# Five pairs of the gated MLP's first product computed by seven quarter products, and five row-pair sums of its last weights moved into the mixer

## The chip, the cores and the metric

The program runs on one core of a Trainium2 chip. The core has five engines that run side by side, each through its own queue of instructions: TensorE (PE in the profile; PEld is its weight load), VectorE (DVE), ScalarE (ACT), GpSimd (POOL) and SyncE (SP, which only issues transfers here). They wait for each other by semaphores. Data lies in SBUF, in 128 partitions; products arrive in PSUM, in banks of 512 columns of float32. The time is that of one execution on the device in microseconds, and the time before is the median of the runs shown.

## The reference

One layer of a streaming encoder on 512 tokens of 1024 channels, in float32: a mixer of four branches (differential attention, forgetting attention, a convolution module, a short gated convolution), a cross-attention, and a gated MLP. The change lies in the MLP, whose lines in the reference are these:

```python
hf = _rms_norm(x, norm_ffn_pre[l])
u = _dwconv_causal(hf @ w_up[l], ffn_dw[l]) + ffn_dw_b[l]
u_g, u_v = jnp.split(u, 2, axis=-1)
yff = (jax.nn.silu(u_g) * u_v) @ w_down[l]
x = x + _rms_norm(yff, norm_ffn_post[l])
```

`w_up` is 1024 x 5632, its first half for the gate, the second for the value; `w_down` is 2816 x 1024; the convolution along the tokens has three taps for each channel.

## The kernel before, in words

Each float32 product is made of three matmuls: every operand is split into a high part (a cast by ScalarE, the tiles `wh`, `hth`) and a low part (the rest, a subtraction by VectorE, the tiles `wl`, `htl`), and high x high, low x high and high x low are summed in PSUM (`mm3`). `split_weights` (L179 to L192) makes the parts of a weight tile of 128 x 1024; in the profile the cast is L190 and the subtraction L191.

The kernel is written as generators of jobs. `run_blocks` takes them in order, loads and splits the weights of the jobs ahead (three of them), and then runs the body of a job. A background list (`bg`) weaves smaller tasks in by an estimated clock. The order of the program's instructions on each engine is then that of the build; each engine works through its own queue strictly in order.

The up-projection is `up_jobs`. There are 22 pairs j of 128 gate and 128 value channels, so 44 jobs, one weight tile of 512 KB each (`wr`, loaded by SP). A job of the plain kind is `channel_major`: 8 blocks of 128 input channels, three matmuls each, 24 matmuls with 512 token columns. Then `done` makes the convolution: the first tap as a ScalarE activation with bias from PSUM into the tile `c`, the other two taps by VectorE from PSUM (`taps`, L594). After the value half of a pair, the gate is made by a Tanh on ScalarE (L1561) and two VectorE instructions (L1562 and L1564), which write a tile `qa` or `qb`. The first two pairs come while the normalised tokens `hth`, `htl` are still being transposed: their first halves of the tokens are computed ahead, and their second halves when `open_ffn` has opened the stage. A bank that holds a product is free for the next product but one only after its last tap.

The second product, `down_jobs`, already works with seven products for each 2 x 2 block of quarters. It needs sums and differences of the quarters of the weights and of the activations. Those of the weights are made by the class `Sums`: `load` fetches two rows of 128 x 1024 of `w_down`, `add` makes four VectorE additions of 128 x 512 (L542 to L545), `store` writes them to DRAM, from where the second product reads them. `up_jobs` does one step of these in each job from the seventh on, on ScalarE's DMA queue, for 11 pairs. Those of the activations are four GpSimd additions of 128 x 256 for each two pairs (`activation_sums`, L566 to L569), issued as soon as the second pair of the two is done.

The mixer is `mixer_jobs`: among others `vf_jobs`, `kv_blocks` and `gate_blocks`, jobs of the same kind with the attention tasks in the background. The residual of the tokens lies in four tiles `res` from the end of the mixer to the end of the kernel.

## Time and profile before

| | us |
|---|---|
| runs shown | 1057.01, 1057.06, 1056.11 (median 1057.01) |
| the profiled execution | 1055.79 |
| its span, first to last instruction | 1054.0 |
| TensorE busy | 1041.7 (99%) |
| VectorE busy | 807.1 (77%) |
| ScalarE busy | 501.9 (48%) |
| GpSimd busy | 184.3 (17%) |

In the profile a line of the timeline gives start, length, engine, line, operation, output and inputs, shape and count, and in brackets the idle time before it with what ended it. A matmul's length in the timeline overlaps the next one's, so what matmuls cost is read from start to start, as in the chain that ended last. Rows with `x11` and two numbers after the bar are groups: busy us and mean ns. The up-projection runs from about 696 us, where the first halves of the first two pairs stand, to about 938 us; the second product follows up to 1044 us.

### The profile page before, as it was taken

The page shows a single profiled execution, that of the slowest core. Times are in us where ns is not written, and L with a number is a line of the kernel's source. Part 1 is how long each engine was busy: PE and PEld are TensorE (multiplying, and loading weights), DVE is VectorE, ACT ScalarE, POOL GpSimd, SP SyncE. Part 2 cuts the span into 40 slices and gives each one's busy share as a digit, 9 for nine tenths or more (in the row PEclk, how much of TensorE's full clock was granted, in tenths as well). Part 3 has the DMA queues.
Part 4 walks back from the last instruction along what each step waited for, and adds up shares of the span by engine and source line. Part 5 has one row for each costly group of instructions (what it writes and reads, how often), then busy time and mean ns, then how long its engine had stood idle before and what let it go on. Part 6 is the DMA issues. An engine that isn't in the chain of part 4 may idle for free.

```text
span 1054.0 us, 14559 instructions
## 1 busy us (share of the span) xinstructions
PE 1041.7 (99%) x5295; PEld 886.8 (84%) x5295; DVE 807.1 (77%) x1280; ACT 501.9 (48%) x823; POOL 184.3 (17%) x309
## 2 busy tenths in 40 slices
PE   9999999999999999999999999999999999999996
PEld 8888888888888988888888899998888888888885
DVE  6899997668667467867487798777878777777795
ACT  5322222277465365655444566554333333355661
POOL 4000000300231233433011031121112111111001
PEclk9999999999999999999999999999999999999998
DMA  8854434742342353232359644135576676626662
GB/s 276 282 168 102 103 100 142 193 109 81 116 140 82 100 161 101 80 100 85 96 172 284 207 132 126 60 111 190 186 243 229 214 233 215 196 81 211 210 188 80
DMA packets 165373, 163.08 MB, mean 155 GB/s; under 512 B 6527, under 2 KB 136172, under 8 KB 165045
## 3 DMA queue, kind: packets, MB, share of 16 engines
q1 hardware_dynamic: 152995, 119.91, 38.0%
q0 software_dynamic: 5824, 19.03, 6.2%
q10 hardware_dynamic: 6482, 23.21, 5.7%
q8 instruction: 42, 0.69, 0.3%
q14 instruction: 30, 0.25, 0.1%
HBM read 139.03 MB, written 23.09 MB: 154 GB/s over the span
## 4 chain that ended last, share of the span: by engine, by line
PE 99%; DVE 0%; ACT 0%; issue 0%; POOL 0%; POOLq 0%; DVEq 0%; ACTq 0%
PE ps_mm L232 51%; PE ps_av L232 31%; PE ps_sc L232 8%; PE ps_tr L232 4%; PE ps_tr L236 2%; PE ps_mm L442 1%; PE ps_av L442 1%; PE ps_mm L384 0%; PE ps_sc L389 0%; DVE o L1710 0%; PE ps_tr L426 0%; POOL st_m L270 0%; POOLq L1816 0%; ACT hth L155 0%; ACT hth L432 0%
## 5 line engine op out<-in xcount | busy, mean ns | idle before, releaser
L190 ACT CAST wh<-wr 128x1024 fp32r<-128x1024 f32 (+1 forms) x142 | 148.8, 1049 | 273.3 <-PE ps_mm L232 175.0
L191 DVE TENSOR_TENSOR wl<-wr,wh 128x1024 fp32r<-128x1024 f32 (+1 forms) x142 | 178.5, 1258 | 79.0 <-ACT wh L190 78.8
L232 PE MATMUL ps_mm<-hth,wh 128*128 128x512 f32 (+1 forms) x592 | 221.1, 380 | 0.2 <-ACT hth L155 0.2
L232 PE MATMUL ps_mm<-htl,wh 128*128 128x512 f32 (+1 forms) x592 | 220.7, 379 | 0.0
L232 PE MATMUL ps_mm<-hth,wl 128*128 128x512 f32 (+1 forms) x592 | 220.6, 379 | 0.0
L232 PE MATMUL ps_av<-htl,wh 128*128 128x512 f32 (+1 forms) x352 | 131.8, 374 | 0.0
L232 PE MATMUL ps_av<-hth,wh 128*128 128x512 f32 (+1 forms) x352 | 131.8, 374 | 0.0
L232 PE MATMUL ps_av<-hth,wl 128*128 128x512 f32 (+1 forms) x352 | 131.6, 374 | 0.0
L232 PEld LDWEIGHTS ps_mm<-hth,wh 128*128 128x128 f32 x592 | 109.6, 188 | 20.4 <-ACT hth L155 0.8
L232 PEld LDWEIGHTS ps_mm<-hth,wl 128*128 128x128 f32 x592 | 109.5, 188 | 20.1
L232 PEld LDWEIGHTS ps_mm<-htl,wh 128*128 128x128 f32 x592 | 109.6, 188 | 19.7
L665 DVE SCALAR_TENSOR_TENSOR y<-y,par,y 128x482 f32<-128x482 f32 (+29 forms) x120 | 83.3, 735 | 0.1
L232 PEld LDWEIGHTS ps_av<-hth,wl 128*128 128x128 f32 x352 | 66.1, 188 | 11.9
L232 PEld LDWEIGHTS ps_av<-hth,wh 128*128 128x128 f32 x352 | 66.2, 188 | 11.8
L232 PEld LDWEIGHTS ps_av<-htl,wh 128*128 128x128 f32 x352 | 66.0, 188 | 11.7
L1613 DVE TENSOR_TENSOR wl<-dw,wh 128x1024 fp32r<-128x1024 f32 x32 | 40.2, 1262 | 13.3 <-ACT wh L1612 13.1
L1612 ACT CAST wh<-dw 128x1024 fp32r<-128x1024 f32 x32 | 33.4, 1051 | 23.4 <-PE ps_tr L232 7.9
L1058 POOL TENSOR_SCALAR fbias<-ck,cq 128x128 f32<-128x128 f32 (+3 forms) x32 | 28.2, 888 | 63.0 <-DVE st L1065 59.7
L1561 ACT ACTIVATE th<-c 128x512 f32<-128x512 f32 x22 | 13.9, 632 | 48.0 <-DVE c L594 48.0
L155 ACT CAST pth<-ps_tr 128x512 fp32r<-128x512 f32 (+3 forms) x56 | 23.5, 448 | 24.7 <-PE ps_tr L236 24.6
L594 DVE SCALAR_TENSOR_TENSOR c<-ps_mm,par,c 128x510 f32<-128x510 f32 (+1 forms) x44 | 32.8, 744 | 0.7
L156 DVE TENSOR_TENSOR ptl<-ps_tr,pth 128x512 fp32r<-128x512 f32 (+3 forms) x56 | 27.5, 512 | 5.9 <-ACT pth L155 5.4
(493 smaller groups left out, 2132.5 us busy)
## 6 DMA issues: line engine op xcount, KB each, us to landing
wr<-in_w_up SPq DMA_DIRECT2D x44, 512.0 KB
wr<-in_w_in SPq DMA_DIRECT2D x38, 512.0 KB
wr<-in_w_gate SPq DMA_DIRECT2D x32, 512.0 KB
wp<-in_w_down ACTq DMA_DIRECT2D x22, 512.0 KB
sums<-wp ACTq DMA_DIRECT2D x22, 512.0 KB
dw<-sums SPq DMA_DIRECT2D x44, 256.0 KB
wr<-in_w_branch SPq DMA_DIRECT2D x16, 512.0 KB
wide<-in_w_out SPq DMA_DIRECT2D x12, 512.0 KB
```

The lines of the kernel that those rows point to most:

```text
L155: A.copy(hi, ps)
L156: V.tensor_tensor(lo, ps, hi.bitcast(F32), ALU.subtract)
L190: order(A.copy(hi, raw[:, :n]))
L191: low.tensor_tensor(lo, raw[:, :n], hi.bitcast(F32), ALU.subtract)
L232: PE.matmul(ps, lhs, rhs, start=start, stop=stop)
L236: PE.transpose(ps, x, ident[:n, :n])
L442: keep(PE.matmul(banks[c][:, :S // 2], w[p == 1][:, k, c * P:(c + 1) * P], ht[p == 2][:, i * 4 + k, :S // 2], start=(i, p, k) == (0, 0, 0) ...
L594: ins = V.scalar_tensor_tensor(dst[:, s:], src[:, :S - s], w(k), dst[:, s:], ALU.mult, ALU.add)
L665: ins = V.scalar_tensor_tensor(dst[:, s:], src[:, :S - s], pc("conv_dw", k * 4 + j), dst[:, s:], ALU.mult, ALU.add)
L1058: G.tensor_scalar(bias[:, :w], ck[j][:, :w], -1.0, cq[:, qt, head:head + 1], ALU.mult, ALU.add)
L1612: A.copy(hi, x)
L1613: V.tensor_tensor(lo, x, hi.bitcast(F32), ALU.subtract)
```

## The change

It has four parts.

First, the pairs 4, 7, 10, 13 and 16 (`SEVEN_AT`) are computed by seven products instead of plain ones. The 128 gate and 128 value columns are the two columns of a 2 x 2 block, the two halves of the input channels its rows, and the two halves of the tokens the other side. Each product is 12 matmuls with 256 token columns. The weights' sums and differences are four VectorE additions of 128 x 512 (L1706 to L1709) on the raw tiles `wg` and `wv`, which come by the same two loads of 512 KB; there are four splits (three of 128 x 1024, one of 128 x 512). The tokens' sums and differences are the same for all five blocks and are made once by `token_terms`: eight GpSimd additions of 128 x 1024, with four splits by ScalarE and VectorE, when the first two pairs are done. A seven-product pair is woven with the plain pair after it (`seven_jobs`). Its results are put together in a tile `u` by four ScalarE copies and three VectorE additions from PSUM; the convolution then reads `u`.

Second, five of the eleven row pairs of `w_down` get their sums in the mixer (`down_early`, `EARLY`), in tiles `y8` and on SP's queue; the other six stay in the up-projection, from pair 5 on.

Third, the sums of the activations are issued from pair 18 on (`quart_sums`), for one or two pairs of quarters at a time, and GpSimd is used as before. The tiles of the terms take the place of the residual, which is written to DRAM (`kept`) and read back in the second product.

Fourth, the gate is a Silu on ScalarE and one VectorE multiplication.

The core of the diff:

```diff
+SEVEN_AT = (4, 7, 10, 13, 16)
+EARLY = 5
...
+        early = down_early()
+        for job in vf_jobs(vf):
+            yield job
+            yield next(early)
...
+        else:
+            SP.dma_start(ns.kept[t * P:(t + 1) * P, :], ns.out[t])
...
+    def token_terms():
+
+        tok = [slice(i * S // 2, (i + 1) * S // 2) for i in range(2)]
+        b = {}
+        for k, t in ((0, 0), (0, 1), (1, 1), (1, 0)):
+            ks = slice(4 * k, 4 * k + 4)
+            x = b[k, t] = ring(name="b").rearrange("p (k c) -> p k c", k=4)
+            G.tensor_tensor(x, ns.hf[0][:, ks, tok[t]].bitcast(F32), ns.hf[1][:, ks, tok[t]].bitcast(F32), ALU.add)
+            if (k, t) == (0, 1):
+                G.tensor_tensor(b[0, 0], x, b[0, 0], ALU.subtract)
+            elif (k, t) == (1, 1):
+                G.tensor_tensor(b[0, 1], x, b[0, 1], ALU.subtract)
+                G.tensor_tensor(x, x, b[0, 0], ALU.subtract)
+            elif (k, t) == (1, 0):
+                G.tensor_tensor(x, x, b[1, 1], ALU.subtract)
+        for i, n in ((0, (0, 0)), (1, (1, 1)), (2, (0, 1)), (3, (1, 0))):
+            split(b[n], *ns.terms[i])
...
+        def gated(c, j):
+            A.activation(c[:, 0], c[:, 0], AF.Silu)
+            V.tensor_tensor(ns.quart[j // 2][:, j % 2 * 2:j % 2 * 2 + 2].rearrange("p a b -> p (a b)"), c[:, 0],
+                            c[:, 1], ALU.mult)
...
-                th = ns.fp.tile([P, S], F32, tag="th", name="th")
-                A.activation(th, c[:, 0], AF.Tanh, scale=0.5)
-                V.scalar_tensor_tensor(th, th, 1.0, c[:, 0], ALU.add, ALU.mult)
...
-                if j % 2:
-                    activation_sums(*x, G)
...
+            def product(ps, name, b, first=True):
+                hi, lo = w[name]
+                for k in range(4):
+                    for i, (w_p, x_p) in enumerate(((hi, b[0]), (hi, b[1]), (lo, b[0]))):
+                        matmul(ps[:, :S // 2], w_p[:, k], x_p[:, k], first and i == k == 0, i == 2 and k == 3,
+                               not first)
...
+            def first_weights():
+                g, v = raws[j]
+                su, s4 = kept["su"], kept["s4"] = ring(name="su"), ns.fp.tile([P, S], F32, tag="s4", name="s4")
+                weights(("A11", "A12"), g)
+                V.tensor_tensor(su[:, :S], v[:, :S], v[:, S:], ALU.add)
+                V.tensor_tensor(su[:, S:], su[:, :S], g[:, :S], ALU.subtract)
+                V.tensor_tensor(v[:, :S], g[:, :S], v[:, :S], ALU.subtract)
+                V.tensor_tensor(s4, g[:, S:], su[:, S:], ALU.subtract)
+                return [()]
...
+            def value(hi, lo):
+                u, ps = kept["u"], bank()
+                half_sums(ps, (hi, lo), range(4))
+                product(x["x"], "S4", old(1, 1), False)
+                A.copy(u[:, 0, 1], x["x"][:, :S // 2])
+                half_sums(ps, (hi, lo), range(4, NK))
+                done(n, 1, ps)
+                product(x["v"], "A22", ns.terms[3], False)
+                add(u[:, 1, 0], x["v"])
...
+                    if (j, i) == (1, 1):
+                        open_ffn()
+                        for m, n, ps, w in held:
+                            (channel_major if m or n else by_pass)(ps, w, ns.hf, slice(S // 2, S))
+                            done(m, n, ps)
+                        token_terms()
+                        load_pair(seven[0])
```

How this stands in the queues, at three places. The names carry a running number of their own in each program.

GpSimd where the up-projection opens: before, the last scale of the normalisation (`st_r`), a load, and then the sums of the activations of the first pairs.

```order
L268 TENSOR_TENSOR st_m_6828<-st_s_6826,nhalf_68 128x1 [waits Activation_49]
L271 TENSOR_TENSOR st_r_6829<-st_m_6828,nhalf_68 128x1 [waits DVE_49,Pool_49]
L1548 DMA g_ffn_7013<-in_norm_ffn_post 128x1024 [waits DMASW5_49,PE_49]
L567 TENSOR_TENSOR qa_6991<-qa_6991 128x256 [waits DVE_49]
L566 TENSOR_TENSOR qa_6991<-qa_6991,qb_6992 128x256 [waits DVE_49]
L568 TENSOR_TENSOR qa_6991<-qa_6991 128x256 [waits Pool_49]
L569 TENSOR_TENSOR qb_6992<-qb_6992,qa_6991 128x256 [waits DMASW1_49,Pool_49]
L567 TENSOR_TENSOR qa_6993<-qa_6993 128x256 [waits DMASW2_49,DVE_49]
```

And with the change:

```order
L270 TENSOR_TENSOR st_m_6876<-st_s_6874,nhalf_68 128x1 [waits Activation_49]
L273 TENSOR_TENSOR st_r_6877<-st_m_6876,nhalf_68 128x1 [waits DVE_49,Pool_49]
L1597 TENSOR_TENSOR b_7172<-hth_6498,htl_6499 128x1024 [waits DMAHW4_49,DMAHW5_49,DMAHW3_49,DMAHW6_49,DMAHW2_49,DMAHW7_49,DMAHW0_49,DVE_49]
L1597 TENSOR_TENSOR b_7174<-hth_6498,htl_6499 128x1024 [waits DVE_49]
L1597 TENSOR_TENSOR b_7177<-hth_6498,htl_6499 128x1024 [waits DVE_49]
L1597 TENSOR_TENSOR b_7181<-hth_6498,htl_6499 128x1024
L1599 TENSOR_TENSOR b_7172<-b_7174,b_7172 128x1024 [waits Pool_49]
L1601 TENSOR_TENSOR b_7174<-b_7177,b_7174 128x1024 [waits Pool_49]
L1602 TENSOR_TENSOR b_7177<-b_7177,b_7172 128x1024 [waits Pool_49]
L1604 TENSOR_TENSOR b_7181<-b_7181,b_7177 128x1024 [waits Pool_49]
L1661 TENSOR_TENSOR t3_8709<-qa_7053 128x256 [waits DMAHW1_49,DVE_49,PE_49]
```

The load is gone, eight additions of 128x1024 stand behind the scale, and the next sums of activations (L1661) are those of the last part of the stage.

VectorE at the same place. `htl` is the low part of the last transposed tokens; `wl_6881` and `wl_6912` belong to the gate and the value job of pair 2, and the L594 rows are the taps of pairs 0 and 1 (`c_7039`, `c_7098`). Before:

```order
L156 TENSOR_TENSOR htl_6456<-ps_tr_6928,hth_6455 128x4x128 [waits Activation_49]
L156 TENSOR_TENSOR htl_6456<-ps_tr_6935,hth_6455 128x4x128 [waits Activation_49]
L191 TENSOR_TENSOR wl_6881<-wr_6878,wh_6880 128x1024 [waits DMAHW0_49,Activation_49]
L594 SCALAR_TENSOR_TENSOR c_7039<-ps_mm_6839,par0_403,c_7039 128x510 [waits PE_49,Activation_49]
L191 TENSOR_TENSOR wl_6912<-wr_6909,wh_6911 128x1024 [waits DMAHW1_49,PE_49,Activation_49]
L594 SCALAR_TENSOR_TENSOR c_7039<-ps_mm_6839,par0_403,c_7039 128x511 [waits DVE_49]
L594 SCALAR_TENSOR_TENSOR c_7039<-ps_sc_6884,par0_403,c_7039 128x510 [waits Activation_49]
L594 SCALAR_TENSOR_TENSOR c_7098<-ps_mm_6915,par0_403,c_7098 128x510 [waits Activation_49]
L594 SCALAR_TENSOR_TENSOR c_7039<-ps_sc_6884,par0_403,c_7039 128x511 [waits DVE_49]
L1562 SCALAR_TENSOR_TENSOR th_7070<-th_7070,c_7039 128x512 [waits Activation_49]
```

With the change, `wl_6929` and `wl_6960` are those of pair 2, L598 are the taps, and `wg_7192`, `wv_7193` the raw weights of pair 4:

```order
L158 TENSOR_TENSOR htl_6499<-ps_tr_6983,hth_6498 128x4x128 [waits Activation_49]
L193 TENSOR_TENSOR wl_6929<-wr_6926,wh_6928 128x1024 [waits DMAHW7_49,Activation_49]
L1706 TENSOR_TENSOR su_7231<-wv_7193 128x512 [waits DMAHW3_49]
L598 SCALAR_TENSOR_TENSOR c_7082<-ps_mm_6887,par0_403,c_7082 128x510 [waits PE_49,Activation_49]
L193 TENSOR_TENSOR wl_6960<-wr_6957,wh_6959 128x1024 [waits DMAHW0_49,PE_49,Activation_49]
L1707 TENSOR_TENSOR su_7231<-su_7231,wg_7192 128x512 [waits DMAHW2_49,DVE_49]
L1708 TENSOR_TENSOR wv_7193<-wg_7192,wv_7193 128x512
L598 SCALAR_TENSOR_TENSOR c_7082<-ps_sc_6932,par0_403,c_7082 128x510 [waits Activation_49]
L598 SCALAR_TENSOR_TENSOR c_7082<-ps_mm_6887,par0_403,c_7082 128x511 [waits DVE_49]
L598 SCALAR_TENSOR_TENSOR c_7139<-ps_mm_6963,par0_403,c_7139 128x510 [waits Activation_49]
L1709 TENSOR_TENSOR s4_7232<-wg_7192,su_7231 128x512 [waits DVE_49]
L193 TENSOR_TENSOR wl_7005<-wr_7002,wh_7004 128x1024 [waits DMAHW4_49,Activation_49]
```

The weight sums of pair 4 (L1706 to L1709) now stand between the splits of pair 2 and the taps, and the last tap of the first gate half (`c_7082<-ps_mm_6887` with 511 columns) follows three of them instead of none.

VectorE in the mixer, in the last attention task of the first branch; L912 and L916 are the same operation, which scales a head's output. Before:

```order
L156 TENSOR_TENSOR ptl_3039<-ps_tr_3040,pth_3038 128x3x128 [waits Activation_49]
L892 RECIPROCAL st8_3047<-st8_3047 128x2 [waits Activation_49]
L893 TENSOR_SCALAR st8_3047<-st8_3047,lam_71 128x1 [waits DVE_49]
L909 TENSOR_REDUCE ms4_3069<-head_fbias_3027 128x4 [waits Activation_49]
L895 SCALAR_TENSOR_TENSOR e_3046<-e_3046,st8_3047 128x512 [waits Activation_49]
L912 TENSOR_TENSOR head_ck_3028<-head_ck_3028,st_r_3072 128x512 [waits DMASW4_49,DMASW5_49,DMASW2_49,DMASW6_49,DMASW1_49,DMASW7_49,DMASW0_49,Pool_49]
L679 STREAM_TRANSPOSE head_fbias_3077<-head_ck_3028 128x512 [waits DVE_49]
```

With the change:

```order
L545 TENSOR_TENSOR y8_3124<-y8_3124 128x512 [waits DMAHW6_49,DMAHW5_49]
L546 TENSOR_TENSOR y8_3124<-y8_3124 128x512 [waits DVE_49]
L896 RECIPROCAL st8_3048<-st8_3048 128x2 [waits Activation_49]
L548 TENSOR_TENSOR y8_3124<-y8_3124 128x512 [waits DVE_49]
L897 TENSOR_SCALAR st8_3048<-st8_3048,lam_71 128x1 [waits DVE_49]
L549 TENSOR_TENSOR y8_3124<-y8_3124 128x512 [waits DVE_49]
L545 TENSOR_TENSOR y8_3125<-y8_3125 128x512 [waits DMAHW7_49,DMAHW0_49]
L899 SCALAR_TENSOR_TENSOR e_3047<-e_3047,st8_3048 128x512 [waits Activation_49]
L546 TENSOR_TENSOR y8_3125<-y8_3125 128x512 [waits DVE_49]
L913 TENSOR_REDUCE ms4_3070<-head_fbias_3028 128x4 [waits Activation_49]
L548 TENSOR_TENSOR y8_3125<-y8_3125 128x512 [waits DVE_49]
L549 TENSOR_TENSOR y8_3125<-y8_3125 128x512 [waits DVE_49]
```

Eight additions of row pairs 0 and 1 (`y8_3124`, `y8_3125`) are woven between the small operations of that task, ahead of the scaling of the head.

239 lines of the change are left out of this document (186 added, 53 removed).

## The prediction

> **What bounds the kernel now.** I read the busy table of the page first, then the chain that ended last, then the windows and the timeline around the stage that is edited.
>
> ```profile
> span 1054.0 us, 14559 instructions
> PE 1041.7 (99%) x5295; PEld 886.8 (84%) x5295; DVE 807.1 (77%) x1280; ACT 501.9 (48%) x823; POOL 184.3 (17%) x309
> PE 99%; DVE 0%; ACT 0%; issue 0%; POOL 0%; POOLq 0%; DVEq 0%; ACTq 0%
> ```
>
> TensorE is busy in 99% of the span and is 99% of the chain that ended last, so time is won by removing TensorE work and lost where TensorE is made to wait. The same holds in the stages that are touched; the columns are the window, the length, then busy us of PE, PEld, DVE, ACT and POOL, with instructions:
>
> ```profile
> 340.00:380.00 40.00, 40.00 (x279) 37.28 (x279) 23.68 (x49) 18.91 (x33) 13.20 (x21) 1.00 0.40 117
> 720.00:800.00 80.00, 80.00 (x358) 66.37 (x357) 63.66 (x80) 31.64 (x39) 15.42 (x16) 1.00 0.62 201
> 800.00:900.00 100.00, 100.00 (x443) 82.81 (x442) 79.15 (x99) 36.59 (x45) 17.26 (x18) 1.00 0.68 223
> ```
>
> PE has no gap in any of the three; DVE runs at 59%, 80% and 79%, so DVE is the engine that can turn into a wait. What PE's work costs is read from the chain, whose pieces run from start to start:
>
> ```profile
> 41.14 5.44 PE ps_mm L232 x24
> 612.22 5.65 PE ps_mm L232 x48
> 634.43 1.36 PE ps_mm L232 x12
> 720.89 0.47 PE ps_av L232 x2
> 721.36 5.45 PE ps_mm L232 x24
> ```
>
> A 512-column matmul costs 5.44/24 = 226.7 ns. A 256-column one costs 5.65/48 = 117.7 ns in one place and 1.36/12 = 113.3 ns in another.
>
> **The change, part by part.**
>
> *The products.* Each of five pairs goes from 48 matmuls of 512 columns (10.88 us) to 84 of 256. Five: 240 x 226.7 ns = 54.4 us leave; 420 arrive. At 117.7 ns they cost 49.4 us, a saving of 5.0; at 113.3 ns, 47.6 us, a saving of 6.8. I take 117.7, because the long run of 48 that follows 512-column work went at it, and the seven products stand between 512-column blocks. Each return from 256 to 512 columns may cost something: the piece at 721.36 took 5.45 us where 24 alone take 5.44, and the weave has about four returns per block, so I allow 0.03 us x 20 = 0.6 us (0 to 1). Sum: -4.4 us (-4.4 to -6.8).
>
> *The token sums.* Eight GpSimd additions of 128x1024 are new, right where the up-projection opens. No row shows that size. GpSimd has 256 and 512 columns:
>
> ```profile
> 723.52 0.73 POOL L567 TENSOR_TENSOR qa<-qa 128x256 f32<-128x256 f32 x1 [17.71 <-DVE qa L1564]
> L415 POOL TENSOR_TENSOR wa<-e,wa 128x512 fp32r<-128x512 f32 x4 | 5.1, 1297 | 1.8 <-ACT wa L412 1.8
> ```
>
> From 0.73 to 1.297 us for 256 more columns gives, as an estimate, 1.30 + 2 x 0.56 = 2.42 us each, 19.4 us in all. GpSimd's last work ahead of them is this one:
>
> ```profile
> 704.72 0.55 POOL L271 TENSOR_TENSOR st_r<-st_m,nhalf 128x1 f32<-128x1 f32 x1
> ```
>
> So the first can begin at about 705.3 us, and the others from 710, when the last transposed quarter is there (below). They are not on PE's path by themselves: their results feed the first seven-product block, which PE reaches at 720.8 + 4 x 5.44 = 742.5 us, 746 with the stall below. But they meet VectorE. These rows are GpSimd (first three) and DVE (last three) at one place:
>
> ```profile
> 791.04 1.12 POOL L566 TENSOR_TENSOR qa<-qa,qb 128x256 f32<-128x256 f32 x1 [10.02 <-DVE qb L1564]
> 792.24 1.07 POOL L568 TENSOR_TENSOR qa<-qa 128x256 f32<-128x256 f32 x1
> 793.38 1.61 POOL L569 TENSOR_TENSOR qb<-qb,qa 128x256 f32<-128x256 f32 x1
> 791.60 1.11 DVE L544 TENSOR_TENSOR wp<-wp 128x512 f32<-128x512 f32 x1
> 792.63 1.76 DVE L191 TENSOR_TENSOR wl<-wr,wh 128x1024 fp32r<-128x1024 f32 x1
> 794.31 1.23 DVE L545 TENSOR_TENSOR wp<-wp 128x512 f32<-128x512 f32 x1
> L543 DVE TENSOR_TENSOR wp<-wp 128x512 f32<-128x512 f32 x11 | 7.6, 688 | 0.2
> ```
>
> Alone, an addition like L544 takes 0.69 us (the row of L543, the same shape), L191 1.23 (below), GpSimd's 0.73. Here the ends run 792.16, 792.71, 793.31, 794.39, 794.99, 795.54: each two-input addition with both inputs in SBUF ends its own length after the other engine's one ended. They take turns, one instruction each. So a VectorE addition of this kind can wait for a whole GpSimd one. What VectorE has to do there before:
>
> ```profile
> 709.30 1.29 DVE L156 TENSOR_TENSOR htl<-ps_tr,hth 128x512 fp32r<-128x512 f32 x2 [2.71 <-ACT hth L155]
> 714.71 1.23 DVE L191 TENSOR_TENSOR wl<-wr,wh 128x1024 fp32r<-128x1024 f32 x1 [4.12 <-ACT wh L190]
> 715.85 0.74 DVE L594 SCALAR_TENSOR_TENSOR c<-ps_mm,par,c 128x510 f32<-128x510 f32 x1
> 716.52 1.23 DVE L191 TENSOR_TENSOR wl<-wr,wh 128x1024 fp32r<-128x1024 f32 x1
> 717.66 0.74 DVE L594 SCALAR_TENSOR_TENSOR c<-ps_mm,par,c 128x511 f32<-128x511 f32 x1
> 718.32 0.74 DVE L594 SCALAR_TENSOR_TENSOR c<-ps_sc,par,c 128x510 f32<-128x510 f32 x1
> ```
>
> The split of 716.52 belongs to the value half of pair 2, which PE begins at 720.8; the tap of 717.66 frees the bank of the first gate half, which the gate half of pair 2 takes over (721.36). Both are some 3 us early. After the change, the queue between 714.7 and that tap is: split, sum of the value weights, tap, split, two weight differences, tap, tap. Own time, from start to start (1.14 from 716.52 to 717.66, 0.66 to the next, and 0.69 less the same 0.08 of overlap): 2 x 1.14 + 3 x 0.61 + 3 x 0.66 = 6.1 us, and five of the eight take turns with GpSimd. Laid out by hand with 2.42 us a turn: GpSimd's third addition ends at 714.9, the split at 716.0; the fourth ends at 718.4, the weight sum at 719.0; the fifth ends at 721.4, the second split at 722.3. PE wants it at 721.2 (third matmul of its block): a stall of 1.1 us. The sixth ends at 724.7, the next difference at 725.2; the seventh at 727.6, the third at 728.1; the two taps end at about 729.3. PE, shifted by 1.1, has 22 matmuls of the value half written ahead of the gate half and wants the bank at 726.8 (725.7 unshifted): a second stall of about 2.4 us. GpSimd is done at about 730. What stands between that and the split of the first seven-product weights is some 13 us of VectorE's own work, so that ends near 744 and is in time for 746, by little. Sum of the opening: **+3.5 us**. Below, it is 0 (no turns taken: the tap ends at 714.7 + 6.1 = 720.8, PE has not asked yet). Above, it is 7: if GpSimd's first addition too begins only at 710, everything after slips by one turn, 2.42 + 1.2 us.
>
> The longest that a VectorE addition is seen to wait is about 0.7 us, beside GpSimd's 1.3 us one:
>
> ```profile
> 13.69 3.12 DVE L191 TENSOR_TENSOR wl<-wr,wh 128x1024 fp32r<-128x1024 f32 x2 [0.26 <-ACT wh L190]
> ```
>
> That is 3.12 for two where 2.4 is usual. If no wait were longer, five would cost 3.5 us, and the tap would end at 724.3, before PE asks: no stall, and a time of 1053.1. The Trainium skill, page "SBUF — State Buffer", section "Who interferes with whom", speaks against that and against the change: the pair of ports that VectorE and GpSimd share is an exclusive lock, held for the full instruction, and a VectorE instruction with two SBUF inputs contends with a GpSimd instruction that reads SBUF. By that rule a wait grows with GpSimd's instruction, the opening costs the 3.5 us above, and the time is 1056.8; the turns at 791 to 795 us agree with it, for instructions up to 1.3 us.
>
> *The rest of a seven-product block.* VectorE gains per block four weight sums (4 x 0.69), one split more (1.23), a half-size one (0.69) and three 256-column additions from PSUM (0.42, as in the row of 355.32 below), 5.9 us. Over the three pairs of a period, one operation of the gate goes in each (3 x 0.69, as for L543), and the row-pair sums fall from two pairs to one (-2.75). From 63.66/80 x 32.6 = 26.0 us that makes 27.1 in 10.88 x 2 + 9.9 = 31.6 us of PE, 86%. No stall, since the weights are split 6 us and more ahead; if that cover went, each late split would show up in full. ScalarE's four copies and one more table load fit in an engine that is idle for 63% of the stage. The weights are the same bytes.
>
> *Row-pair sums in the mixer.* Twenty additions of 0.69 us move to about 342 to 380 us, together with 20 DMAs of 512 KB on the SP queue, among weight loads. VectorE goes from 23.7 to 37.4 of 40 us. Its longest gaps there are these:
>
> ```profile
> 355.32 0.42 DVE L156 TENSOR_TENSOR v<-ps_mm,v 128x256 fp32r<-128x256 f32 x1 [4.79 <-ACT v L155]
> 369.18 1.23 DVE L191 TENSOR_TENSOR wl<-wr,wh 128x1024 fp32r<-128x1024 f32 x1 [2.42 <-ACT wh L190]
> ```
>
> The additions fill such gaps, in groups of two to four (1.4 to 2.7 us), and the weights behind them are split a job ahead. GpSimd's 13.2 us in the window take turns with them too. I take +0.3 us; from 0 to 3.5, the second if half of GpSimd's 13.2 us is waited for on VectorE, which then needs 44 of 40 us.
>
> *The activation sums.* The 44 GpSimd additions of 256 columns, spread over the stage before (16 to 17 us per 80 to 100), are issued from the last seven-product block on, up to eight per 5.44 us job, so they take turns with the splits of the last pairs. GpSimd needs 44 x 0.82 = 36 us (0.74 and the 0.08 between 792.16 and 792.24), and the first sums are wanted when the second product starts. I take +0.2 us (0 to 2). The later gain vector and the residual written out and read back lie behind 100% PE windows: nothing, or a few tenths at the end if the read came late.
>
> The sum: -4.4 + 3.5 + 0.3 + 0.2 = -0.4 us. The profiled execution took 1055.79 us (span 1054.0), 1.2 less than the median of the runs, 1057.01; against that median the forecast is 1056.6, which a measurement cannot tell from no change: I take 0.2%, or 2.1 us, as what it can tell.
>
> **The rivals.**
>
> *The sums on GpSimd are hidden.* If the turns are not so strict for the long additions, or VectorE gets its splits in before them, the opening costs under 1 us. Against it: the rows at 791. The time is 1057.0 - 4.4 + 0.5 = 1053.1.
>
> *The small matmuls run at 113.3 ns.* The run at 634 did. With the opening in full that is 1056.6 - 1.8 = 1054.8; together with the first rival, 1051.3.
>
> *The opening stalls for longer (slower).* One mechanism: GpSimd's first addition cannot start at 705, since its output lies in memory that the stage has only just opened, and all eight fall behind 710. The second stall then grows by one turn: +7.1 in the opening, 1060.2 in all. It decides from about 2.5 us of extra delay. For it speaks that the addition is told to wait for seven DMA queues; against it, that those are loads of long before.
>
> *VectorE is overfull in the mixer (slower).* With the 3.5 us of the bound above, 1059.8. The window of 340 to 380 would show PE idle behind a split or a query part.
>
> **How the numbers follow.** The forecast, an opening of 2 to 5 us and little else: 0.32. Hidden opening: 0.24. Faster small matmuls with the opening as forecast: 0.11. Longer opening: 0.19. Overfull mixer: 0.11. Something else, either way: 0.03. The last is shared equally. Faster by over 0.2% are the second and the third (that one barely): 0.36. Within 0.2%: 0.33. Slower: 0.31. The range reaches from 1052.0, most of the way to both gains together, to 1061.0, just above the longer opening; the forecast's own range is 1055 to 1058.5.
>
> **What would show it.** Right: PE's instructions rise by 180; the matmul steps of the seven products read 5.65 per 48; GpSimd's eight rows of 128x1024 stand between 705 and 731 at 2.4 us and more, VectorE's splits among them are drawn out to 2 or 3 us, and PE has two gaps at 721 and 727, released by DVE, of 3.5 us in sum. Wrong: no gap of PE before 740 (first rival), gaps inside the seven-product blocks, or gaps between 340 and 380. A VectorE that is over 95% busy from 745 to 900 would break my claim that the blocks are covered, and a gap at about 935 that of the activation sums.

## The result, and the profile after

The changed kernel takes 1063.24 us (median of four runs, 1062.15 to 1064.95) against 1056.56 us before (four runs): a ratio of 1.0065, with a 95% interval of 1.0048 to 1.0082. It is slower, by 5 to 9 us, where 1056.6 us and "no change that can be told" was forecast, and outside the range (1052.0 to 1061.0).

The page of the profiled execution after (1064.95 us), its span, its busy engines and the chain that ended last:

```profile
span 1063.2 us, 15056 instructions
PE 1040.3 (98%) x5475; PEld 891.6 (84%) x5475; DVE 833.7 (78%) x1329; ACT 522.4 (49%) x880; POOL 217.0 (20%) x317
PE 83%; DVE 6%; DMA 6%; issue 2%; ACT 2%; POOL 1%; SPq 0%; DVEq 0%; POOLq 0%; ACTq 0%
```

TensorE's instructions rise by 180 as expected, but it is busy 23 us less than the span, and 17% of the chain now lies on other engines and on transfers. TensorE's waits by what ended them, a view that groups each kind (total, times, longest):

```profile
PE ps_mm L234 <- DVE qk L815: 2.8, 1, 2.8
PE ps_mm L234 <- DVE c L598: 2.2, 1, 2.2
PE ps_av L234 <- DVE wl L193: 2.0, 2, 1.2
PE ps_sc L234 <- ACT hth L1817: 1.8, 1, 1.8
PE ps_mm L386 <- DVE e L337: 1.3, 1, 1.3
PE ps_tr L238 <- DVE nt L283: 0.7, 1, 0.7
PE ps_tr L238 <- DVE par L500: 0.6, 1, 0.6
```

The row of L386 was there before. The last one lies at 28 us, comes and goes between kernels, and made 0.5 us here. The others stand in three places: the mixer (`qk`, one of the `wl`), the opening of the up-projection (`nt`, the other `wl`, `c`) and the start of the second product (`hth`). To put lengths to them I compare when the same matmul starts in both traces. Its delay is 0.5 us before the mixer's stage at 345 us and 6.9 after it; so **the mixer loses 6.4 us** (6.3 in the expectations below). The gaps in the opening add 0.8 + 1.35 + 2.3 = **4.5 us**, that at the second product **1.9 us**. With the 0.5 at 28 us these are 13.3, and the span grew by 9.2: the rest, **4.1 us, is the saving** of the seven products. These sizes are those of one execution on each side, and the one after is the slowest of its four: the medians differ by 6.7 us.

### The profile page after: what moved, and what is told of

The parts are those of the page before. It is cut to its first block, busy times and chain, and to the rows that moved or that the text cites. A ratio compares the mean times of both kernels' runs of the same rounds, so it can differ in the third digit from the quotient of the medians.

```text
span 1063.2 us, 15056 instructions
## 1 busy us (share of the span) xinstructions
PE 1040.3 (98%) x5475; PEld 891.6 (84%) x5475; DVE 833.7 (78%) x1329; ACT 522.4 (49%) x880; POOL 217.0 (20%) x317
## 4 chain that ended last, share of the span: by engine, by line
PE 83%; DVE 6%; DMA 6%; issue 2%; ACT 2%; POOL 1%; SPq 0%; DVEq 0%; POOLq 0%; ACTq 0%
PE ps_mm L234 43%; PE ps_av L234 23%; PE ps_sc L234 10%; PE ps_tr L234 4%; PE ps_tr L238 2%; DVE wl L193 2%; DMA y<-in_w_down 2%; DMA wr<-in_w_up 1%; DMA wp<-in_w_down 1%; DVE c L598 1%; DMA dw<-sums 1%; DMA wr<-in_w_in 1%; DMA wide<-in_w_out 1%; DVE nt L283 1%; ACT wh L192 1%
## 5 line engine op out<-in xcount | busy, mean ns | idle before, releaser
L192 ACT CAST wh<-wr 128x1024 fp32r<-128x1024 f32 (+1 forms) x132 | 138.2, 1049 | 231.6 <-PE ps_mm L234 125.7
L193 DVE TENSOR_TENSOR wl<-wr,wh 128x1024 fp32r<-128x1024 f32 (+1 forms) x132 | 166.9, 1266 | 84.4 <-ACT wh L192 83.7
L234 PE MATMUL ps_mm<-hth,wh 128*128 128x512 f32 (+1 forms) x552 | 206.3, 381 | 5.2 <-DVE qk L815 2.8
L234 PE MATMUL ps_mm<-htl,wh 128*128 128x512 f32 (+1 forms) x552 | 205.7, 380 | 0.0
L234 PE MATMUL ps_mm<-hth,wl 128*128 128x512 f32 (+1 forms) x552 | 205.6, 379 | 0.0
L234 PE MATMUL ps_av<-hth,wl 128*128 128x512 f32 (+1 forms) x312 | 116.3, 373 | 2.0 <-DVE wl L193 2.0
L234 PE MATMUL ps_av<-hth,wh 128*128 128x512 f32 (+1 forms) x312 | 116.3, 373 | 0.0
L234 PE MATMUL ps_av<-htl,wh 128*128 128x512 f32 (+1 forms) x312 | 116.2, 373 | 0.0
L1661 POOL TENSOR_TENSOR t<-qa 128x256 f32<-128x256 f32 x10 | 7.8, 779 | 158.8 <-PE ps_sc L234 150.4
L1619 ACT ACTIVATE c<-c 128x512 f32<-128x512 f32 x22 | 13.9, 632 | 39.9 <-DVE c L598 39.9
L234 PE MATMUL ps_mm<-y8b,wh 128*128 128x512 f32 x96 | 30.4, 395 | 0.0
```

Of the source, the lines that this page charges most:

```text
L192: order(A.copy(hi, raw[:, :n]))
L193: low.tensor_tensor(lo, raw[:, :n], hi.bitcast(F32), ALU.subtract)
L234: PE.matmul(ps, lhs, rhs, start=start, stop=stop, skip_group_check=more)
L1619: A.activation(c[:, 0], c[:, 0], AF.Silu)
```

## The experiments

Times are medians; a ratio is to the kernel before on the same chip. "The mixer loses" is the growth of a matmul's delay between about 345 and 530 us, read as above.

**The mixer and the opening, one at a time.** Without the early row pairs:

```diff
-        order = [[(f.load, 0)], [(f.load, 1)], [], [(f.add, 0, 0), (f.add, 0, 1), (f.store, 0)],
...
+        order = []
```

> The five early row pairs are left out of the mixer: no load, no addition, no store of them; the second product reads plain quarters of w_down in their place, with as many bytes, so its values are others. The trace of the changed kernel puts TensorE 6.3 us behind between 355 and 405 us. If that is all owed to the early row pairs, it goes, with the lower granted clock (0.83 in 390 to 400 us): 1063.2 - 6.3 = 1057 us, and no gap of TensorE between 340 and 420. If part of it comes from something else in the changed program there, a gap stays and the time is 1059 or more.

Measured: 1057.86 us, 1.0021 (1.0007 to 1.0035). The mixer loses 0.0 us; all of it is owed to the early row pairs. The opening's gaps stay (0.7, 1.35 and 2.3 us).

The token sums in four pieces each:

```diff
-            G.tensor_tensor(x, ns.hf[0][:, ks, tok[t]].bitcast(F32), ns.hf[1][:, ks, tok[t]].bitcast(F32), ALU.add)
+            for k in range(4):
+                G.tensor_tensor(x[:, k], ...[:, k], ...[:, k], ALU.add)
```

> The eight GpSimd additions of the token sums are cut into 32 of 128x256, the same elements. If a VectorE addition waits for the end of one GpSimd instruction, a wait falls from 2.4 to 0.7 us at most, and the opening's three gaps (0.8, 1.35 and 2.3 us) go nearly all: 1059 us. The sums are then done at about the same time or some 4 us later. If what counts is the time in which GpSimd reads at all, however it is cut, the gaps stay: 1063.

Measured: 1059.53 us, 1.0036 (1.0025 to 1.0047). The three gaps are gone. VectorE's timeline in the opening of the changed kernel, and two of GpSimd's instructions there:

```profile
712.24 3.42 DVE L283 SCALAR_TENSOR_TENSOR nt<-res,st_r,g_pre 128x1024 f32<-128x1024 f32 x1 [0.92 <-POOL st_r L273]
723.62 2.88 DVE L1706 TENSOR_TENSOR su<-wv 128x512 f32<-128x512 f32 x1
727.08 2.76 DVE L193 TENSOR_TENSOR wl<-wr,wh 128x1024 fp32r<-128x1024 f32 x1
729.76 2.88 DVE L1707 TENSOR_TENSOR su<-su,wg 128x512 f32<-128x512 f32 x1
732.56 2.87 DVE L1708 TENSOR_TENSOR wv<-wg,wv 128x512 f32<-128x512 f32 x1
```

```profile
712.17 2.40 POOL L1597 TENSOR_TENSOR b<-hth,htl 128x1024 f32<-128x1024 f32 x1
725.91 2.85 POOL L1599 TENSOR_TENSOR b<-b 128x1024 f32<-128x1024 f32 x1
```

And with the small additions, the same split and the two additions around it:

```profile
723.39 1.22 DVE L1711 TENSOR_TENSOR su<-wv 128x512 f32<-128x512 f32 x1
725.19 1.80 DVE L193 TENSOR_TENSOR wl<-wr,wh 128x1024 fp32r<-128x1024 f32 x1
726.91 1.22 DVE L1712 TENSOR_TENSOR su<-su,wg 128x512 f32<-128x512 f32 x1
```

With the same elements in smaller instructions, a VectorE addition of 0.69 us takes 1.22 instead of 2.88: the wait goes with the length of GpSimd's single instruction. That is what the Trainium skill states in "SBUF — State Buffer", section "Who interferes with whom" (a lock held for the whole instruction), now seen up to 2.4 us.

Both together, that is both edits above in one kernel:

> The early row pairs are left out of the mixer (plain quarters of w_down are read in their place) and the token sums are cut into 32 small GpSimd additions. What is left of the change is the seven products, the late activation sums and the gate. If the two losses are the mixer and the opening and they add up, TensorE is about 4.2 us ahead of the kernel before at the start of the second product, and with the gap of 0.5 to 2.1 us seen there the time is 1056.2 - 4.2 + 0.5 to 2.1 = 1052.5 to 1054. If the saving of the seven products is not real, it is 1056 or more.

Measured: 1052.31 us, 0.9962 (0.9947 to 0.9977): faster than before. The saving is real. By the medians, each against before on its own chip, leaving out one loss saves 5.0 and 3.3 us, and both together 10.5; why that is 2.2 us more than the sum was not found. One gap of 1.6 us is left, at the second product.

**What in the mixer costs it.** Four kernels take one ingredient each out of the early row pairs, and a fifth moves the transfers; the opening is left as in the changed kernel. First the additions:

```diff
+        order = [[g for g in steps if g[0] != f.add] for steps in order]
```

> The early row pairs are still loaded and stored in the mixer, but their 20 VectorE additions are left out (the stored rows are not summed). Theory one: the additions hold VectorE, and the splits behind them come late: without them the gaps go, 1057 us. Theory two: the 20 transfers are the cause, by bandwidth (308 GB/s in 340 to 380 us) and by weight loads standing behind stores on SP's queue: the gaps stay for the most part, 1060 us or more. I hold theory two for the larger share: two of TensorE's waits go back to a transfer of wr that was issued late or took 5 to 6 us.

Measured: 1059.16 us, 1.0026 (1.0016 to 1.0036). The mixer loses 1.6 us: the transfers alone are a small part, so "theory two" is wrong as it stands.

Additions of one column in place of 512, behind the same loads and ahead of the same stores:

```diff
-            (b11, b12), (b21, b22) = ((x[:, :S], x[:, S:]) for x in self.held[q])
+            n = 1 if q < EARLY and self.pairs == NF // 2 else S
+            (b11, b12), (b21, b22) = ((x[:, :n], x[:, S:S + n]) for x in self.held[q])
```

> The changed kernel with the 20 early additions made on one column instead of 512 (the stored rows are not summed), at the same places, behind the same loads and ahead of the same stores; all transfers stay. Without any addition the mixer lost 1.7 us, with all 6.3, with all additions but four of ten loads 1.1. If the cost is that VectorE's queue stands still while an addition waits for its load, and that stores and weight loads stand behind that on SP's queue, most of it stays: 4 to 6 us, in all 1061 to 1063. If it is VectorE's 13.7 us of work beside the transfers, it falls to about 2: 1058 to 1059.5.

Measured: 1060.59 us, 1.0043 (1.0027 to 1.006). The mixer loses 2.0 us: the waits alone do not make the loss; the additions' length is needed. The waits are not quite the same, though: behind such short additions the stores and the next loads go out earlier too.

All additions and stores, but only two row pairs loaded:

```diff
+        def again(q):
+            f.held[q] = [next(free) for _ in range(2)]
+
+        order = [[(again, g[1]) if g[0] == f.load and g[1] > 1 else g for g in steps] for steps in order]
```

> In the mixer only row pairs 0 and 1 are loaded; pairs 2, 3 and 4 are added and stored from what lies in the two tiles, so all 20 additions and all ten stores stay and six of ten loads go (the sums of three pairs are others). If VectorE's 13.7 us of additions cost the time, the mixer still loses about 4.6 us: 1061 to 1063. If what costs is that an addition stands in VectorE's queue waiting for a load that is under way for 8 us, and the loads and stores on SP's queue behind each other, most of the 6.3 us goes: 1058 to 1059.

Measured: 1059.35 us, 1.0033 (1.0021 to 1.0046). The mixer loses 1.2 us, though VectorE does all 20 additions: its busy time is no cause alone either.

The stores left out:

```diff
+        order = [[(f.held.pop, n[0]) if g == f.store else (g, *n) for g, *n in steps] for steps in order]
```

> All ten early loads and 20 early additions stay in the mixer, the ten stores are left out (the second product reads plain quarters of w_down in their place). Where the mixer loses 6.3 us in full, 1.7 without additions, 2.0 with additions of one column and 1.1 with four of ten loads, two accounts are left. One: what costs is the loads' landing late under VectorE's additions, stores do not matter: 4 us or more stay, 1060 to 1062. Two: what costs is the crowd of transfers together with the stores that hold up SP's queue behind the additions: it falls to 0 to 2, 1057 to 1058.5.

Measured: 1060.36 us, 1.0044 (1.0029 to 1.0059). The mixer loses 2.4 us, between the two accounts.

So each of the three, taken out, leaves 1.2 to 2.4 of 6.4 us. The kernel with small token sums has the same mixer as the changed one and lost 7.0 us there, so a few tenths between two of these kernels say nothing. The largest gap shows how the three meet. SP's queue around it, in the kernel before and then in the changed one:

```profile
377.10 0.37 SPq L176 DMA_DIRECT2D wr<-in_w_branch  x1
```

```profile
381.46 1.89 SPq L553 DMA_DIRECT2D sums<-y  x2
384.96 0.38 SPq L178 DMA_DIRECT2D wr<-in_w_branch  x1
```

The load of the branch weights stands behind two stores, but it is not they that it waits for last: the second is out at 383.35 us (381.46 and 1.89), and the load goes 1.6 us later, as soon as a split ends. Weight loads go through two raw tiles `wr`, and a load needs the tile that a split of VectorE sets free. What made that split late lies 20 us earlier, in VectorE's queue; the same split before, and then with the addition that came before it in the changed kernel:

```profile
361.97 1.23 DVE L191 TENSOR_TENSOR wl<-wr,wh 128x1024 fp32r<-128x1024 f32 x1 [1.61 <-ACT wh L190]
```

```profile
361.73 0.69 DVE L545 TENSOR_TENSOR y<-y 128x512 f32<-128x512 f32 x1 [3.66 <-DMA y<-in_w_down]
365.73 1.22 DVE L193 TENSOR_TENSOR wl<-wr,wh 128x1024 fp32r<-128x1024 f32 x1
```

VectorE stood idle for 3.66 us in front of an addition whose load had not landed. This addition and four more then stand ahead of the split, whose cast was done at 362.46. The split comes 3.3 us late (less the 0.5 of before), and with it the weight load that takes its tile. The weight load after that one stands on SP's queue behind an early load, which waits until a store has landed:

```profile
370.29 0.33 SPq L540 DMA_DIRECT2D y<-in_w_down  x1
370.66 0.43 SPq L178 DMA_DIRECT2D wr<-in_w_in  x1
```

Its tile was free at 368.69, so here SP's queue costs 2.0 us. And the three weight loads from 367 to 376 us are under way for 6.2, 6.6 and 6.2 us, where the same three took 4.9, 5.2 and 4.1 before, with 308 GB/s in 340 to 380 us in place of 117. Followed back along its own tile, the branch load is 7.4 us late: 3.5 by the first weight load (nearly all of it the late split), 3.4 by two longer transfers and 0.5 by VectorE's queue once more. The stores that stand just ahead of it add nothing. The chain after it in the changed kernel, in order of time:

```profile
384.96 5.24 DMA wr<-in_w_branch
390.20 0.02 issue
390.22 1.05 ACT wh L192
391.28 0.02 issue
391.30 0.67 DVE wl L193
...
392.56 0.70 DVE qk L815
393.26 0.14 issue
393.40 3.03 PE ps_mm L234 x9
```

The split of these weights stands in VectorE's queue ahead of a query part (`qk`) that TensorE wants next. Less the delay that each run had before the mixer, the load is issued 7.4 us late in the changed kernel, and 4.9, 4.2, 3.2 and 2.8 us late without additions, with tiny ones, without later loads and without stores. In these four the gap behind a query part there is 0.6 to 1.2 us, in the changed kernel 3.0 us. So 2 to 4 us of the lateness are hidden in each, as an estimate from these differences, and all three ingredients together go well beyond that. The traces also show what each takes away: without additions, or with tiny ones, the first weight load goes within 0.1 us of its time; without stores it is under way for 4.0 us in place of 6.2.

Moving the transfers off SP:

```diff
-        ns.sums = Sums(w_down, NF // 2, lambda: next(free), SP, "sums")
+        ns.sums = Sums(w_down, NF // 2, lambda: next(free), A, "sums")
```

> The early row pairs are loaded and stored through ScalarE's queue instead of SP's; additions and bytes stay. If the order on SP's queue is the cause (a weight load behind a store that waits for an addition), weight loads are issued on time and at most 2 of the 6.3 us stay: 1057 to 1059. If it is bandwidth or VectorE, nothing changes: 1063. A third way: ScalarE's own work stands behind stores that wait for VectorE, and the loss grows.

Measured: 1065.04 us, 1.0082 (1.0064 to 1.01). The mixer loses 5.4 us, and the branch load is still 7.5 us late, with no early transfer on SP's queue: the first weight load goes 3.4 us late, again behind its split. So the lateness does not need the order on SP's queue. Some waits are new, on `y8b` of ScalarE among others: ScalarE did nothing for 6.2 us before 360.7 us, its casts behind early loads that wait until a store has landed. That is the third way of the expectation, in part.

**Spreading the additions.** Three kernels with small token sums have the next load of the late row pairs ahead of an addition:

```diff
+            yield ns.sums.load, EARLY
             for q in range(EARLY, NF // 2):
-                yield ns.sums.load, q
+                yield ns.sums.load, q + 1
```

The first has three early row pairs, each added two steps or more after its load, and takes two steps for the late ones in a seven-product block (`step(2)` in `second`):

> All outputs as the reference: three early row pairs instead of five, each added two jobs or more after its load; the token sums in 32 small additions; in the up-projection the next load stands ahead of an addition, and the second product of each seven-product block takes two steps. By my account: the saving of 4.2 us, minus 0 to 2 in the mixer, minus 0.5 to 2 at the second product: 1052.5 to 1056, faster than the kernel before. If VectorE's additions cost wherever they stand, the mixer loses 12/20 of 4.6 = 2.8 us and VectorE stalls TensorE in the up-projection too: 1057 or more.

Measured: 1065.57 us, 1.0083 (1.0059 to 1.0106). The mixer loses 3.6 us, but the up-projection and the second product lose 3.7, 1.9 and 2.2 us at 907, 948 and 951 us.

The second has all five, in this order:

```diff
+        order = [[(f.load, 0)], [(f.load, 1)], [], [], [(f.add, 0, 0)], [(f.add, 0, 1), (f.store, 0)], [(f.add, 1, 0)],
+                 [(f.add, 1, 1), (f.store, 1)], [(f.load, 2)], [(f.load, 3)], [], [(f.add, 2, 0)],
...
```

> As v1 with all five early row pairs, in 20 steps instead of 13, each added two jobs or more after its load, and one step per seven-product block. If an addition that waits for its load is the cause, the mixer loses 0 to 2 us: 1053 to 1056. If the additions' own time or the bytes are the cause, it loses 4 or more: 1058 or more.

Measured: 1059.23 us, 1.0029 (1.0018 to 1.004). The mixer still loses 6.5 us: the branch load goes at 384.73, 7.6 us late, again as soon as a split ends. The weight load ahead of it on the other tile still stands behind an early load (370.22 and 370.60 on SP's queue).

The third queues each transfer behind the latest weight load and each addition behind the latest split, over 22 steps:

```diff
+            for g, *n in steps:
+                with tc.issue_after(mark["low" if g == f.add else "SP"]):
+                    g(*n)
```

> All outputs as the reference. All five early row pairs in the mixer, the same additions and bytes, but spread over 22 steps, each transfer queued on SP behind the latest weight load and each addition on VectorE behind the latest split; a store stands a step after its addition. Token sums in 32 small additions, next load ahead of an addition in the up-projection. If the mixer's loss is weight loads that come late because early loads and stores stand ahead of them and crowd them (up to 309 GB/s for 40 us), it falls from 6.5 us to 0 to 1.5: 1052 to 1054, faster than the kernel before. If the bytes and additions cost wherever they stand, it stays at 1058 or more.

Measured: 1061.22 us, 1.0049 (1.0036 to 1.0063). From 345 to 530 us it loses 5.7 us in many small pieces, with one gap of 2.3 us ahead of a task of the forgetting attention, and 1.8 more by 640 us, though the branch load is only 0.6 us late. I found no place for five row pairs in the mixer that does not cost; that there is none is not shown.

**The second product.** The kernel without early row pairs and with small token sums again, with the edit of the late loads shown above:

> As the kernel without early row pairs and with small token sums (1052.3 us, one gap of 1.6 us where the second product starts), and with the next load of the late row pairs standing ahead of an addition. If that gap comes from the late row pairs, whose last load, addition and store end only when the second product wants its own weights, it goes: 1050.7 us. If it comes from the split of the activations in two pieces or from the order of ScalarE's work, it stays: 1052.3.

Measured: 1052.01 us, 0.996 (0.9947 to 0.9974). The gap falls from 1.6 to 0.3 us, but a new one of 0.6 appears at 750 us, and the median does not tell the two apart. The chain that leads to the gap in the changed kernel goes through the last late row pair; three of its pieces, the load, its first addition and the split that stands behind it on VectorE:

```profile
924.62 9.89 DMA wp<-in_w_down
934.60 0.69 DVE wp L545
936.50 1.69 DVE wl L1818
```

So the late row pairs can hold up the second product, by way of a load that is under way for 9.9 us. They do not always: of the nine kernels with these row pairs in the order of the changed one, two (without additions and without later loads) show no such gap, and the others 0.3 to 2.0 us. How much of the fall from 1.6 to 0.3 is the edit's is not shown.

**A version with all outputs.** All row pairs in the up-projection, five of the eleven on GpSimd:

```diff
-EARLY = 5
+EARLY = 0
...
+                yield ns.sums.load, q + 1
+                yield (ns.sums.add_g if q % 2 == 0 and q < 10 else ns.sums.add), q
```

> All outputs as the reference. No row pair is summed in the mixer; all eleven are summed in the up-projection, the first, third, fifth, seventh and ninth by GpSimd (which has nothing to do from 745 to 888 us) in additions of 128x256, the others by VectorE; token sums in 32 small additions. If the mixer's loss is owed to the early row pairs alone and VectorE has room in the up-projection (86% by my count, plus waits for GpSimd of 0.7 us at most), the saving of the seven products is left: 1051.5 to 1054, faster than the kernel before. If VectorE's turns with GpSimd or the memory ring shared by raw weights and row pairs hold TensorE up, 1056 or more, with gaps between 760 and 900 us.

Measured: 1065.33 us, 1.0086 (1.0071 to 1.0101). The mixer loses nothing; there are gaps of 3.2 us at 749 and 6.3 us at 901 us. The second one, by VectorE's timeline, and by the start of GpSimd's run:

```profile
889.80 17.70 DVE L193 TENSOR_TENSOR wl<-wr,wh 128x1024 fp32r<-128x1024 f32 x1 [0.21 <-ACT wh L192]
```

```profile
889.80 2.12 POOL L1675 TENSOR_TENSOR qa<-t,qa 128x256 f32<-128x256 f32 x3
891.89 0.73 POOL L1673 TENSOR_TENSOR t<-qa 128x256 f32<-128x256 f32 x1
892.59 0.73 POOL L1674 TENSOR_TENSOR t<-qa 128x256 f32<-128x256 f32 x1
```

A split of 1.2 us took 17.7, through a run of GpSimd additions that follow each other 0.70 us apart without a wait. The next version starts the row pairs at pair 4, gives GpSimd the odd ones, and keeps the activation sums in program order, so that two of each four wait for the one before:

```diff
+                    with tc.issue_after(st["chain"]) if "chain" in st else ExitStack():
+                        st["chain"] = G.tensor_tensor(*args).ins
```

> All outputs as the reference. No early row pair; all eleven in the up-projection from pair 4 on, five of them added by GpSimd; GpSimd's activation sums in the order of the program, two independent ones and then two that wait for the one before, in place of up to eleven independent ones in a row. If the split of 17.7 us at 890 us came from GpSimd additions that follow each other without a wait, no VectorE instruction is longer than 3 us there and the gap of 6.3 us goes; with the gap at 749 us (row-pair sums beside the token sums) gone too: 1052 to 1054. If such a split is met again, 1056 or more.

Measured: 1053.25 us (nine runs), 0.9972 (0.9962 to 0.9982): **faster than both kernels**, with all of the computation. Its page and the start of its list of TensorE's waits:

```profile
span 1051.8 us, 15103 instructions
PE 1038.1 (99%) x5475; PEld 890.7 (85%) x5475; DVE 829.3 (79%) x1309; ACT 522.9 (50%) x880; POOL 270.4 (26%) x381
```

```profile
PE ps_mm L386 <- DVE e L337: 1.3, 1, 1.3
PE ps_sc L234 <- DVE wl L193: 0.7, 1, 0.7
PE ps_tr L238 <- DVE par L500: 0.6, 1, 0.6
```

No VectorE addition from 700 to 1000 us is longer than 1.8 us. The gap at 749 us is down to 0.9. Since three things changed at once, which of them took the long split away is not shown.

With four seven-product pairs and all row pairs on VectorE:

```diff
-SEVEN_AT = (4, 7, 10, 13, 16)
+SEVEN_AT = (4, 8, 12, 16)
```

> All outputs as the reference. Four seven-product pairs (4, 8, 12, 16) in place of five, no early row pair, all eleven added by VectorE in the up-projection, GpSimd's activation sums in the order of the program. Saving 4/5 of 4.2 = 3.4 us. If VectorE carries it (about 88% busy), 1053 to 1054.5; if late row pairs hold up the second product, 1055 to 1056.5.

Measured: 1056.07 us, 1.0003 (0.9992 to 1.0014). Its profiled execution took 1053.55 us and shows one gap of 1.1 us; the other nine runs lie between 1053.9 and 1058.1. What the longer ones lose isn't in that trace: inconclusive.

## Why the prediction was wrong

**The step that failed** is "Row-pair sums in the mixer ... I take +0.3 us; from 0 to 3.5". It measured 6.4 us. It was priced by VectorE's busy time (37.4 of 40 us), and the range by GpSimd's turns, on the ground that the additions fill gaps and "the weights behind them are split a job ahead". The window after:

```profile
340.00:380.00 40.00, 39.14 (x274) 36.49 (x274) 28.10 (x60) 15.93 (x30) 8.06 (x14) 1.00 0.90 308
```

VectorE was busy for 28.1 us, not 37.4: it was not full, it waited, and part of its work slipped past the window. With all additions and few loads the loss is 1.2 us. What was missed is what the moved work stands ahead of and waits for: an addition that waits for its load puts the splits behind it off (3.3 us), the weight loads wait for those splits and then take longer among 20 more transfers (3.4 us for two of them), and SP's queue holds one of them for 2.0 us. The rival "VectorE is overfull in the mixer" had the place and the sign, with the wrong mechanism and half the price.

Part of the 6.4 us is not waiting. The four gaps from 365 to 391 us sum to 4.7. The windows after the longest one, two us each, with the granted clock as the third number from the end:

```profile
394.00:396.00 2.00, 2.00 (x8) 1.58 (x7) 1.93 (x4) 1.10 (x2) 0.85 (x3) 0.69 1.03 292
396.00:398.00 2.00, 2.00 (x6) 1.51 (x6) 0.84 (x2) 1.12 (x2) 0.35 (x2) 0.50 0.82 256
```

In these 4 us TensorE loses 0.31 x 2 + 0.50 x 2 = 1.6 us by its clock. The prediction had no price for that. In all the traces (from 100 us on, idle times as the profile gives them) a loss by the clock followed six of the seven gaps of 2.4 us or more, and two of the ten of 1.9 to 2.2 us. It was 1.6 to 1.7 us each time, and 2.4 after the gap of 6.2 us.

**The opening** was right in mechanism and nearly in size. Forecast were GpSimd instructions of 2.42 us (2.40 alone), stalls of 1.1 and 2.4 us at 721 and 727 (1.35 and 2.3, at the same places once the delay from before is taken off). Missed was a third of 0.8 us: the normalisation `nt` (3.42 us for 1.28) also takes turns, since GpSimd's first addition starts 0.07 us ahead of it. So 4.5 where +3.5 was forecast. The turns at 791 us that this was read from end 0.1 to 0.15 us short of the instructions' own lengths, as the layout by hand then took them. Added up by its own steps that layout gives stalls of about 1.4 and 2.9 us, not 1.1 and 2.4, and the 1056.8 given for this opening should be 1056.6 by the prediction's own sum.

**The products** saved 4.1 us where 4.4 was forecast, at 118 ns a matmul as taken:

```profile
753.93 1.41 PE ps_sc L234 x12
756.76 2.75 PE ps_mm L234 x12
760.43 2.50 PE ps_sc L234 x22
```

The first is 117.5 ns each, the last 113.6; the twelve of 512 columns between take 2.75 us instead of 2.72, which is the 0.03 of a return. Runs at 113 ns exist, but the matmuls of 256 columns between 742 and 885 us average 117.5 ns from start to start, so that rival falls. The range given for the saving (-4.4 to -6.8) left out the allowance for the returns, up to 1 us, at its lower end: it should start at -4.0.

**The activation sums** were put at +0.2 (0 to 2) and 1.9 was lost at the second product, by another way: the chain there goes through the late row pairs, not through GpSimd. Since this gap varies from 0 to 2.0 us among kernels with the same late row pairs, its size is partly chance. **The rest of the seven-product blocks** holds: no gap from 750 to 945 us, with VectorE busy 115.1 of 140 us (82%, 86% forecast). "The sums on GpSimd are hidden" and "the opening stalls for longer" both fall; the sign that decided came from the mixer.

Put together: -4.1 + 4.5 + 6.4 + 1.9 + 0.5 = 9.2 us, against -4.4 + 3.5 + 0.3 + 0.2.

## What to carry to other kernels

Before work is moved into a stage because its engines have idle time, write down for each queue what the moved transfers and waits stand ahead of. An addition that waits for its load holds every split behind it, and a transfer that waits for a store holds every load behind it. Then follow the tiles: a late split makes the next weight load late. Give the engine that shares its memory port with another many small instructions instead of few large ones; the two versions in which they also wait for each other now and then had no split held through a whole run, but other things differed too, and most versions without it had none either. And expect 1.6 to 1.7 us more, for the clock, after most TensorE stalls of 2.4 us or more.

## What the runs showed of the hardware that was not expected

- VectorE can be kept off the port for a whole run of GpSimd instructions, not for one: splits of 8.8, 9.7 and 17.7 us were met in three kernels, beside 12, 13 and 24 GpSimd additions that follow each other about 0.70 us apart (early transfers on ScalarE's queue, three early row pairs, and five row pairs on GpSimd). TensorE then stood idle for 2.4, 3.5 and 6.2 us. In most other kernels the same run let VectorE in after each instruction, so the order of starts seems to matter; what decides it was not found.
- The granted clock fell to 0.5 to 0.7 for some 4 us after gaps of 3.0 and 3.3 us in the mixer (the changed kernel and the one with all five row pairs in 20 steps). After the 2.3 us gap of the opening it fell in the kernel without early row pairs (0.70 in 732 to 736 us) and not in the changed one, whose gap is as long. After a gap of 3.7 us at 907 us, in the kernel with three early row pairs, it did not fall. The Trainium skill, "TensorE: Matmul & The Clock Gate", Part 1, puts the loss of the clock after about one idle window of 3.4 us; here 2.3 us, with the 1.35 us gap 6 us before it, was enough once and not enough once, and 3.7 us was not enough once. So no threshold follows from these gaps.
- A wait can move to another queue with the transfers: with the early ones on ScalarE's queue, ScalarE did nothing for 6.2 us behind loads that wait for stores, and the mixer's loss stayed (5.4 us for 6.4).
